# Splitting each 128x1024 weight tile with one ScalarE and one VectorE operation, two buffers each, in a two-layer hybrid model

## The chip, the core and the metric

The kernel runs on one core of one Trainium2 chip. The core has TensorE (PE, the matmuls; PEld is its loading of weights), VectorE (DVE), ScalarE (ACT), GpSimd (POOL) and SyncE (SP), whose queue issues the DMAs here. The engines run side by side, each through its own instructions in a fixed order, and wait for each other by semaphores. The metric is the device time of one execution in microseconds (us), as the median of several runs.

## What is computed

Two layers of a diffusion backbone on 256 context tokens and 256 latent tokens with 2048 channels. Cut to what matters (`ctx` and `x` are one array of 512 columns in the kernel):

```python
for l in range(2):
    u = rmsnorm(x, norm_w) * (1 + scale) + shift          # shift, scale, gate = silu(c) @ ada_w + ada_b
    lx, lg, q, k, v, ag, xbc, z, dt = split(u @ w_in)      # 2048 x 7184 weights
    lru = rglru(dwconv(lx)) * silu(lg)                     # two scans over the tokens
    att = window_attention(rope(rmsnorm(q)), rope(rmsnorm(k)), v) * silu(ag)
    ssd = rmsnorm(ssd_chunked(silu(dwconv(xbc)), dt) * silu(z))
    x = x + gate * (concat(lru, att, ssd) @ w_out)         # 3072 x 2048 weights
```

The second layer gives only the latent tokens. There the columns of `lg`, `q`, `ag`, `z`, `C` and the output projection are 256 wide; those of `B`, `x`, `lx`, `k`, `v`, and all of the first layer, are 512 wide.

## The kernel before

All weights are float32. To multiply them as float32r and keep their precision, each is split into two parts of 12 bits: `hi`, its value rounded by ScalarE into float32r, and `lo`, the rest, which VectorE subtracts. Each block of 128x128 weights then takes three matmuls in `mm3`: `hi` by `u_hi`, `hi` by `u_lo`, and `lo` by `u_hi`.

The weights lie in HBM as tiles of 128x1024 (512 KB), eight blocks each, in the order in which they are used: 112 tiles of `w_in` and 48 of `w_out` for each layer, 320 in all. The generator `blocks` streams them. For each tile it asks for a buffer `raw` (one of three), has SP load it (L232), and then for each of its two halves asks for a buffer `hi` and one `lo` (one of `HB` = 3 each, 128x512), gives ScalarE the rounding (L237) and VectorE the subtraction (L238), and yields the four blocks of the half. So 640 halves go through ACT and DVE. A buffer `hi` or `lo` comes free when TensorE is done with the half in it, a buffer `raw` when `lo` of its second half is computed. All matmuls go through L174; the three of a block are named `acc<-u,hi`, `acc<-u,hi` and `acc<-u,lo` (`mx` in place of `acc` for some column tiles).

`layer` runs, for each layer: the column tiles `B`, `C` and part of `x`, with the channel tiles outermost; the remaining `x`; eight pairs `lx`, `lg` (two tiles each), beside which the SSD's core runs; eight `z`; `k` and `v`; eight pairs `q`, `ag`; and the output projection in three thirds of 16 tiles each, one tile for one row block `m`, after which VectorE adds the gated result to `x` (L1073). The order of TensorE is that of the program: between two blocks `pump` puts in what the mixers need, when a clock of estimated matmul times says that it is due. The order on ACT, DVE, POOL and SP is set by a scheduler, which simulates the program when it is built; at run time each engine keeps to it. The mixers share those engines with the split: L380 (products for adaLN, on DVE, weights `araw` loaded by SP at L377), L1162 and L1166 (the SSD's weight matrices `ee`, `ww`), L730 to L735 (the LRU's scans), L650 and L654 (the gate of `z`), and loads and stores of `lru` and `att` through DRAM (L750, L900, L918, L1078).

Of the kernel before, what the change touches and what calls it, by code (L numbers as in the profile page):

```python
# [8 lines left out]
F32 = mybir.dt.float32  # L9
F32R = mybir.dt.float32r  # L10
AF = mybir.ActivationFunctionType
ALU = mybir.AluOpType
AX = mybir.AxisListType

P = 128
# [15 lines left out]
# The order in which the column tiles of w_in are multiplied: the first ones with the channel tiles outermost, those in  # L31
# FILL a few channel tiles at a time between them (in the first layer, whose adaLN weights take the DMAs' time).
HEAD = [[("B", 0), ("B", 1), ("C", 0), ("C", 1), ("x", 0), ("x", 1)]] * 2
FILL = [[("x", i) for i in range(2, 6)], []]
# [3 lines left out]
ROWS = (14, 11)  # the channel tiles multiplied one by one; the column tiles end one behind the other  # L38


def head_plan(l):
    """[(column tile, its channel tiles)] in order"""
# [21 lines left out]
def lead(at):  # L64
    """how many steps of the adaLN's rows go before the product of channel tile int(at)"""
    return int(np.interp(at, *LEAD)) // 2 * 2
# [26 lines left out]
OUT_PARTS = (0, 2, 1)  # lru, ssd, att: thirds of the rows of w_out  # L93
# [18 lines left out]
# Tiles of different phases that share their places.  # L112
SHARED = {}
for _tag, _bufs, _roles in [
        ("raw", 3, ("raw",)),
# [16 lines left out]
HB = 3  # L132
# [7 lines left out]
class Kernel:  # L140
# [52 lines left out]
    def wait(self, name):  # L193
        """how long, on TensorE's clock, to leave other engines for the step named"""
        return WAIT[name][self.l]
# [32 lines left out]
    def blocks(self, src, n_tiles):  # L228
        nc = self.nc
        for i in range(n_tiles):  # L230
            raw = self.t([P, 8, P], "raw")
            nc.sync.dma_start(out=raw, in_=src[i].rearrange("p (b c) -> p b c", b=8))  # L232
            for h in range(2):
                hi = self.t([P, 4, P], "hi", HB, F32R)
                lo = self.t([P, 4, P], "lo", HB, F32R)
                part = raw[:, 4 * h:4 * h + 4]
                nc.scalar.activation(out=hi, in_=part, func=AF.Copy)  # L237
                nc.vector.tensor_tensor(out=lo, in0=part, in1=hi.bitcast(F32), op=ALU.subtract)  # L238
                for b in range(4):
                    yield hi[:, b], lo[:, b]  # L240
# [8 lines left out]
    def setup(self):  # L249
# [25 lines left out]
        # 1/sqrt of the mean square of each token, on all partitions  # L275
# [1000 lines left out]
```

## Time and profile before

| | |
|---|---|
| median of 3 runs (lowest to highest) | 1871.07 us (1868.7 to 1872.88) |
| span of the profiled execution, the only time that its page gives | 1873.5 us |
| TensorE, matmuls | 1786.4 us busy, 95% |
| VectorE | 1474.5 us, 79% |
| ScalarE | 908.2 us, 48% |
| GpSimd | 438.0 us, 23% |
| mean granted TensorE clock | 0.981 of 2.4 GHz |

The busy share of TensorE is modelled from pipelined matmuls, so the idle time between them and the pace of a stream of blocks say more than the share. The stages differ in what is wide and what runs beside them, so the pace is read for each stage by itself.

### The profile page before, as it was taken

Reading aid. Unit: us, or ns where it says so; the run is one execution under the profiler, and the core shown is the slowest. Engines: PE = TensorE matmul, PEld = TensorE weight load, DVE = VectorE, ACT = ScalarE, POOL = GpSimd, SP = SyncE. Lnnn points to the kernel's source line nnn. Section 1 sums busy time; section 2 is a strip of 40 time slices with the busy share of each in tenths; the row PEclk is TensorE's granted clock in tenths of the full one; section 3 lists DMA queues with packets and bytes.
Section 4 is the critical chain, followed back from the end, with each engine's and each line's share of the span. In section 5 each row is a group of like instructions: output and inputs, shape, how many; then the busy total and the mean of one; then the engine's idle time right before and its main releaser. Section 6 shows DMA issues by size and latency. Waiting matters only on the chain.

```text
span 1873.5 us, 29483 instructions
## 1 busy us (share of the span) xinstructions
PE 1786.4 (95%) x10458; PEld 1493.3 (80%) x10458; DVE 1474.5 (79%) x3101; ACT 908.2 (48%) x1590; POOL 438.0 (23%) x467
## 2 busy tenths in 40 slices
PE   7999998887999999999999999999989899999999
PEld 4777876665767888887888887888767788999999
DVE  4447879899898888899999546877898895788765
ACT  4324565554633354546332234534656663677543
POOL 0000246665210022221100021011374430232000
PEclk9999999989999999999999998999999999999999
DMA  9982332333565655556766433354333555554666
GB/s 379 365 280 68 117 107 88 104 102 112 200 219 191 191 169 163 173 181 204 253 222 220 143 122 106 124 198 155 107 99 99 149 194 172 159 179 159 207 192 180
DMA packets 140259, 320.98 MB, mean 171 GB/s; under 512 B 14000, under 2 KB 41552, under 8 KB 139472
## 3 DMA queue, kind: packets, MB, share of 16 engines
q1 hardware_dynamic: 140112, 319.10, 52.0%
q8 instruction: 82, 1.34, 0.3%
q14 instruction: 65, 0.53, 0.1%
HBM read 308.41 MB, written 10.63 MB: 170 GB/s over the span
## 4 chain that ended last, share of the span: by engine, by line
PE 62%; DVE 10%; DMA 3%; issue 2%; ACT 2%; POOL 2%; SPq 0%; DVEq 0%; POOLq 0%; ACTq 0%
PE acc L174 52%; PE mx L174 8%; DVE lo L238 3%; DMA araw<-in_adaw_dram 1%; PE mx L170 1%; DVE ada L380 1%; DVE araw L380 1%; DVE ee L1162 1%; DVE ww L1166 1%; DMA raw<-in_w_in_dram 1%; POOL prob L864 0%; DMA bc<-acsD 0%; DVE xc L466 0%; ACT hi L237 0%; POOL ww L1164 0%
## 5 line engine op out<-in xcount | busy, mean ns | idle before, releaser
L174 PE MATMUL acc<-u,hi 128*128 128x512 f32 (+1 forms) x4800 | 1279.8, 355 | 8.6 <-ACT hi L237 4.2
L174 PEld LDWEIGHTS acc<-u,hi 128*128 128x128 f32 x4800 | 841.8, 191 | 135.0 <-issue 12.5
L174 PE MATMUL acc<-u,lo 128*128 128x512 f32 (+1 forms) x2400 | 847.6, 353 | 30.5 <-DVE lo L238 30.1
L237 ACT ACTIVATE hi<-raw 128x512 fp32r<-128x512 f32 x640 | 399.0, 628 | 607.6 <-PE acc L174 468.7
L238 DVE TENSOR_TENSOR lo<-raw,hi 128x512 fp32r<-128x512 f32 x640 | 471.9, 740 | 191.3 <-ACT hi L237 180.0
L174 PEld LDWEIGHTS acc<-u,lo 128*128 128x128 f32 x2400 | 457.3, 191 | 103.1 <-DVE lo L238 43.1
L380 DVE SCALAR_TENSOR_TENSOR araw<-araw,adac 128x512 f32<-128x512 f32 x256 | 187.0, 731 | 3.9 <-DMA araw<-in_adaw_dram 1.6
L380 DVE SCALAR_TENSOR_TENSOR ada<-araw,adac 128x512 f32<-128x512 f32 x192 | 146.4, 762 | 10.7 <-DMA araw<-in_adaw_dram 7.6
L427 POOL TENSOR_TENSOR ssq<-ssq,sq 128x512 f32<-128x512 f32 (+1 forms) x26 | 33.7, 1298 | 303.6 <-ACT sq L423 303.6
L864 POOL TENSOR_SCALAR prob<-prob,qrs 128x512 f32<-128x512 f32 (+1 forms) x48 | 60.8, 1279 | 187.4 <-ACT hi L237 142.6
L174 PE MATMUL mx<-u,hi 128*128 128x512 f32 (+1 forms) x320 | 99.7, 395 | 0.0
L1073 DVE SCALAR_TENSOR_TENSOR X<-acc,mod,X 128x256 f32<-128x256 f32 x144 | 65.2, 479 | 41.0 <-PE acc L174 40.7
L511 POOL TENSOR_SCALAR X<-xs,prm 128x512 f32<-128x512 f32 (+1 forms) x16 | 14.5, 908 | 323.3 <-DVE xs L489 323.3
L1174 POOL TENSOR_TENSOR bc<-bc,CT 128x512 f32<-128x512 f32 x40 | 59.3, 1483 | 37.4 <-ACT bc L1173 23.7
L174 PEld LDWEIGHTS mx<-u,hi 128*128 128x128 f32 x320 | 56.6, 191 | 14.1 <-issue 4.0
L1162 DVE SCALAR_TENSOR_TENSOR ee<-bc,nacs,ee 128x128 f32<-128x128 f32 x96 | 55.7, 624 | 14.8 <-DMA bc<-acsD 11.8
L767 POOL TENSOR_TENSOR qw<-qw,cst 128x256 f32<-128x256 f32 x20 | 22.4, 1118 | 191.3 <-DVE rt L766 122.1
L174 PE MATMUL mx<-u,lo 128*128 128x512 f32 (+1 forms) x160 | 61.0, 381 | 0.0
L1160 POOL TENSOR_SCALAR ee<-bc,nacs 128x128 f32<-128x128 f32 x96 | 50.0, 532 | 45.6 <-DMA bc<-acsD 31.6
L719 POOL TENSOR_TENSOR la<-lt 128x512 f32<-128x512 f32 x32 | 37.9, 1184 | 95.3 <-ACT lt L717 65.4
L727 POOL TENSOR_TENSOR lt<-lt,ltl 128x512 f32<-128x512 f32 x32 | 47.4, 1500 | 50.2 <-ACT ltl L724 36.3
L711 ACT ACTIVATE lt<-mx,gbh 128x512 f32<-128x512 f32 x64 | 43.0, 684 | 18.8 <-PE mx L174 18.1
(243 smaller groups left out, 2108.6 us busy)
## 6 DMA issues: line engine op xcount, KB each, us to landing
raw<-in_w_in_dram SPq DMA_DIRECT2D x224, 512.0 KB, 3.6
araw<-in_adaw_dram SPq DMA_DIRECT2D x256, 256.0 KB, 3.1
raw<-in_w_out_dram SPq DMA_DIRECT2D x96, 512.0 KB, 3.7
ar<-in_ada_dram SPq DMA_DIRECT2D x84, 256.0 KB, 5.9
bc<-acsD SPq DMA_DIRECT2D x48, 256.0 KB, 4.0
ar<-in_ada_dram SPq DMA_DIRECT2D x22, 512.0 KB, 7.3
adac<-condD SPq DMA_DIRECT2D x28, 256.0 KB, 4.8
X<-in_xT_dram SPq DMA_DIRECT2D x2, 2048.0 KB, 8.0
```

The source lines that it names most:

```text
L174: self.nc.tensor.matmul(out=out, lhsT=lhsT, rhs=rhs, start=start, stop=stop, **kw)
L237: nc.scalar.activation(out=hi, in_=part, func=AF.Copy)
L238: nc.vector.tensor_tensor(out=lo, in0=part, in1=hi.bitcast(F32), op=ALU.subtract)
L380: i = nc.vector.scalar_tensor_tensor(out=o, in0=raw, scalar=1.0, in1=row[c].rearrange("p t x -> p (t x)"), op0=ALU.mult, op1=ALU.mult, acc ...
L711: nc.scalar.activation(out=t, in_=pg, func=AF.Tanh, scale=0.5, bias=self.gb[:, 16 * g + 8 * d + m:16 * g + 8 * d + m + 1])
L719: nc.gpsimd.tensor_tensor(out=a2, in0=tr, in1=tr, op=ALU.mult)
L727: nc.gpsimd.tensor_tensor(out=ti, in0=ti, in1=tl[:, d], op=ALU.mult)
L864: nc.gpsimd.tensor_scalar(out=pr[j], in0=pr[j], scalar1=rs[:, j:j + 1], scalar2=1.0, op0=ALU.mult, op1=ALU.mult)
L1073: nc.vector.scalar_tensor_tensor(out=x[:, s], in0=acc[:, s.start - w0:s.stop - w0], scalar=mod[:, 2 * KT + m, c:c + 1], in1=x[:, s], op0=A ...
L1160: nc.gpsimd.tensor_scalar(out=e[:, j], in0=bcs[0][:, j], scalar1=1.0, scalar2=k.nacs[:, f:f + 1], op0=ALU.mult, op1=ALU.add)
L1162: nc.vector.scalar_tensor_tensor(out=e[:, j], in0=bcs[1][:, j], scalar=k.nacs[:, r:r + 1], in1=e[:, j], op0=ALU.add, op1=ALU.min)
L1174: nc.gpsimd.tensor_tensor(out=bc, in0=bc, in1=k.CT[:, g, None, tok].to_broadcast([P, 4, P]), op=ALU.mult)
```

## The change

The inner loop over halves goes. One operation of ScalarE rounds the whole 128x1024 tile, one of VectorE subtracts it, and the tile's eight blocks are yielded. The tiles `hi` and `lo` are twice as large and have two buffers (`HB` = 2) in place of three; `raw` has two in place of three. The space is the same: 3 x 4 KB + 2 x 3 x 2 KB = 24 KB a partition before, 2 x 4 KB + 2 x 2 x 4 KB = 24 KB after. The rest of the diff takes out comments and docstrings, which moves line numbers by up to two: L237, L238 of before are L235, L236 of after.

```diff
-        ("raw", 3, ("raw",)),
+        ("raw", 2, ("raw",)),
...
-HB = 3
+HB = 2
...
             nc.sync.dma_start(out=raw, in_=src[i].rearrange("p (b c) -> p b c", b=8))
-            for h in range(2):
-                hi = self.t([P, 4, P], "hi", HB, F32R)
-                lo = self.t([P, 4, P], "lo", HB, F32R)
-                part = raw[:, 4 * h:4 * h + 4]
-                nc.scalar.activation(out=hi, in_=part, func=AF.Copy)
-                nc.vector.tensor_tensor(out=lo, in0=part, in1=hi.bitcast(F32), op=ALU.subtract)
-                for b in range(4):
-                    yield hi[:, b], lo[:, b]
+            hi = self.t([P, 8, P], "hi", HB, F32R)
+            lo = self.t([P, 8, P], "lo", HB, F32R)
+            nc.scalar.activation(out=hi, in_=raw, func=AF.Copy)
+            nc.vector.tensor_tensor(out=lo, in0=raw, in1=hi.bitcast(F32), op=ALU.subtract)
+            for b in range(8):
+                yield hi[:, b], lo[:, b]
```

The matmuls and their order on TensorE stay. On the other engines the scheduler places things anew. On VectorE in the last third of the second layer's output projection there stood, for each tile `raw_N`, two halves and the gated addition of the tile before it (`acc`):

```order
L238 TENSOR_TENSOR lo_18508<-raw_18505,hi_18507 128x512
L238 TENSOR_TENSOR lo_18524<-raw_18505,hi_18523 128x512
L1073 SCALAR_TENSOR_TENSOR X_17111<-acc_18467,mod_33_146,X_17111 128x256
L238 TENSOR_TENSOR lo_18545<-raw_18542,hi_18544 128x512
L238 TENSOR_TENSOR lo_18561<-raw_18542,hi_18560 128x512
L1073 SCALAR_TENSOR_TENSOR X_17111<-acc_18504,mod_33_146,X_17111 128x256
```

Now there stands one subtraction for each addition:

```order
L236 TENSOR_TENSOR lo_17247<-raw_17244,hi_17246 128x1024
L1071 SCALAR_TENSOR_TENSOR X_16023<-acc_17210,mod_33_146,X_16023 128x256
L236 TENSOR_TENSOR lo_17280<-raw_17277,hi_17279 128x1024
L1071 SCALAR_TENSOR_TENSOR X_16023<-acc_17243,mod_33_146,X_16023 128x256
L236 TENSOR_TENSOR lo_17313<-raw_17310,hi_17312 128x1024
```

The addition for a tile keeps its place, ahead of the subtraction for the tile after the next.

On VectorE in the second layer's `z` tiles, where the LRU's last scans (`lh`), the gate of `z` (`cv`, then `X`) and the adaLN products (`araw`) share the engine, there stood before:

```order
L238 TENSOR_TENSOR lo_14614<-raw_14611,hi_14613 128x512
L650 SCALAR_TENSOR_TENSOR cv_14566<-cth_14565,acc_14496 128x256
L733 SCALAR_TENSOR_TENSOR lh_3050_14429<-lt_3045_14410,lt_3047_14416 128x256
L238 TENSOR_TENSOR lo_14630<-raw_14611,hi_14629 128x512
L654 SCALAR_TENSOR_TENSOR X_11270<-X_11270,cv_14566 128x256
L735 SCALAR_TENSOR_TENSOR lh_3050_14429<-lt_3045_14410,lh_3050_14429,lt_3047_14416 128x256
L238 TENSOR_TENSOR lo_14657<-raw_14654,hi_14656 128x512
L238 TENSOR_TENSOR lo_14673<-raw_14654,hi_14672 128x512
L380 SCALAR_TENSOR_TENSOR araw_14682,adas_11245<-araw_14682,adac_14026 128x512
L238 TENSOR_TENSOR lo_14694<-raw_14691,hi_14693 128x512
```

and for the same tiles now:

```order
L236 TENSOR_TENSOR lo_13714<-raw_13711,hi_13713 128x1024
L648 SCALAR_TENSOR_TENSOR cv_13670<-cth_13669,acc_13608 128x256
L731 SCALAR_TENSOR_TENSOR lh_2610_13549<-lt_2605_13530,lt_2607_13536 128x256
L652 SCALAR_TENSOR_TENSOR X_10594<-X_10594,cv_13670 128x256
L733 SCALAR_TENSOR_TENSOR lh_2610_13549<-lt_2605_13530,lh_2610_13549,lt_2607_13536 128x256
L236 TENSOR_TENSOR lo_13753<-raw_13750,hi_13752 128x1024
L378 SCALAR_TENSOR_TENSOR araw_13774,adas_10573<-araw_13774,adac_13174 128x512
L648 SCALAR_TENSOR_TENSOR cv_13742<-cth_13741,acc_13677 128x256
L652 SCALAR_TENSOR_TENSOR X_10594<-X_10594,cv_13742 128x256
L236 TENSOR_TENSOR lo_13786<-raw_13783,hi_13785 128x1024
```

What stood between two halves of a tile now stands between two whole tiles, four operations in a row.

On SP in the same place, with the loads of adaLN weights (`araw`) and of the stored `lru` (`ltl`, `stage`), there stood:

```order
L232 DMA raw_14654<-in_w_in_dram 128x1024
L377 DMA araw_14866<-in_adaw_dram 128x512
L232 DMA raw_14691<-in_w_in_dram 128x1024
L918 DMA ltl_16944<-lruD_11533 128x2x256
L918 DMA stage_16946<-lruD_11533 128x256
L232 DMA raw_14734<-in_w_in_dram 128x1024
L918 DMA stage_16948<-lruD_11533 128x256
```

and now, where `raw_13750` is the tile that was `raw_14654`, and `raw_13783` the one that was `raw_14691`:

```order
L232 DMA raw_13750<-in_w_in_dram 128x1024
L375 DMA araw_13942<-in_adaw_dram 128x512
L916 DMA ltl_15864<-lruD_10845 128x2x256
L916 DMA stage_15866<-lruD_10845 128x256
L232 DMA raw_13783<-in_w_in_dram 128x1024
L916 DMA stage_15868<-lruD_10845 128x256
```

The loads of weights slip back by about one tile among the other DMAs.

## Rows read from the trace of the kernel before

**Rows 1.** From the page: TensorE's busy line, and its granted clock in 40 slices.

```profile
PE 1786.4 (95%) x10458; PEld 1493.3 (80%) x10458; DVE 1474.5 (79%) x3101; ACT 908.2 (48%) x1590; POOL 438.0 (23%) x467
...
PEclk9999999989999999999999998999999999999999
```

**Rows 2.** Idle time by engine and releaser: us in total, times, longest us.

```profile
PE acc L174 <- DVE lo L238: 30.1, 27, 3.8
...
SPq L232 <- DVE lo L238: 745.7, 251, 12.3
```

**Rows 3.** Rounding (L237) by stretch: ACT busy (x operations), granted clock, DMA share, GB/s.

```profile
0.00:150.00 150.00, 20.07 (x32) 0.98 0.88 323
...
1498.00:1556.00 58.00, 20.68 (x34) 1.00 0.61 201
1603.00:1726.00 123.00, 40.02 (x64) 1.00 0.54 172
1750.00:1870.00 120.00, 50.98 (x81) 1.00 0.63 191
```

**Rows 4.** All engines by stretch: PE, PEld, DVE, ACT, POOL busy, clock, DMA share, GB/s.

```profile
260.00:600.00 340.00, 303.63 (x1453) 235.88 (x1451) 308.38 (x580) 163.02 (x252) 167.35 (x192) 0.95 0.45 146
...
1300.00:1498.00 198.00, 178.20 (x1024) 147.17 (x1023) 170.94 (x265) 123.86 (x193) 93.54 (x107) 0.96 0.36 115
1498.00:1556.00 58.00, 53.28 (x408) 50.53 (x408) 49.63 (x79) 38.09 (x65) 19.78 (x17) 1.00 0.61 201
```

**Rows 5.** Timeline, second layer's output projection: start us, us, engine, [idle before <-releaser].

```profile
1800.90 0.40 PE L174 MATMUL acc<-u,hi 128*128 128x256 f32 x2
...
1801.14 0.28 PE L174 MATMUL acc<-u,lo 128*128 128x256 f32 x1
...
1800.98 0.63 ACT L237 ACTIVATE hi<-raw 128x512 fp32r<-128x512 f32 x1 [0.81 <-PE acc L174]
1802.42 0.63 ACT L237 ACTIVATE hi<-raw 128x512 fp32r<-128x512 f32 x1 [0.81 <-PE acc L174]
...
1801.11 0.48 DVE L1073 SCALAR_TENSOR_TENSOR X<-acc,mod,X 128x256 f32<-128x256 f32 x1 [0.21 <-PE acc L174]
1801.65 0.69 DVE L238 TENSOR_TENSOR lo<-raw,hi 128x512 fp32r<-128x512 f32 x1
1803.09 0.69 DVE L238 TENSOR_TENSOR lo<-raw,hi 128x512 fp32r<-128x512 f32 x1 [0.75 <-ACT hi L237]
...
1795.17 29.13 SPq L232 DMA_DIRECT2D raw<-in_w_out_dram  x11
```

**Rows 6.** Groups by shape: busy us, mean ns; last row: 1498 to 1556 us.

```profile
L820 ACT ACTIVATE qh<-qw 128x512 fp32r<-128x512 f32 x8 | 5.0, 630 | 8.0 <-POOL qw L768 8.0
L820 ACT ACTIVATE qh<-qw 128x256 fp32r<-128x256 f32 x8 | 3.3, 416 | 5.8 <-POOL qw L768 5.8
...
L821 DVE TENSOR_TENSOR ql<-qw,qh 128x512 fp32r<-128x512 f32 x8 | 5.5, 683 | 0.0
L821 DVE TENSOR_TENSOR ql<-qw,qh 128x256 fp32r<-128x256 f32 x8 | 3.4, 424 | 2.2 <-ACT qh L820 2.2
...
L238 DVE TENSOR_TENSOR lo<-raw,hi 128x512 fp32r<-128x512 f32 x34 | 28.2, 843 | 7.8 <-ACT hi L237 7.8
```

**Rows 7.** DMA issues: KB each, median us to landing; page, then 1500 to 1556 us.

```profile
raw<-in_w_out_dram SPq DMA_DIRECT2D x96, 512.0 KB, 3.7
...
raw<-in_w_in_dram SPq DMA_DIRECT2D x17, 512.0 KB, 4.3
```

**Rows 8.** Timeline of ACT, first layer's output projection, 512 columns wide.

```profile
1071.12 0.63 ACT L237 ACTIVATE hi<-raw 128x512 fp32r<-128x512 f32 x1 [1.22 <-PE acc L174]
1073.83 0.63 ACT L237 ACTIVATE hi<-raw 128x512 fp32r<-128x512 f32 x1 [2.08 <-PE acc L174]
```

**Rows 9.** Timeline of DVE among the second layer's `z` tiles.

```profile
1530.24 2.30 DVE L730 TENSOR_TENSOR_SCAN lh<-lt,lt 128x512 f32<-128x512 f32 x1
1532.46 1.14 DVE L238 TENSOR_TENSOR lo<-raw,hi 128x512 fp32r<-128x512 f32 x1
...
1536.04 1.26 DVE L238 TENSOR_TENSOR lo<-raw,hi 128x512 fp32r<-128x512 f32 x2
```

## The prediction, made before the changed kernel was run

> **What bounds the kernel now.** I read the page's busy line first: TensorE is busy 95% of the span, and its granted clock stands at nine tenths or more in every slice [rows 1]. So the kernel is a stream of blocks through TensorE, and an edit to the splitting can only take away what TensorE waits for, or make it wait. The list of waits says how much there is to take: `acc` waits for `lo` 27 times, 30.1 us in all; the loads of `raw` wait on SP for `lo` 251 times, which is the queue waiting for a free buffer and costs nothing as long as the tile lands in time [rows 2]. The question is thus which of the rings of buffers is the next to be late, and that is read from one tile's timeline where nothing else runs.
>
> That place is the second layer's output projection [rows 5]. The roundings of two halves start 1.44 us apart, each released by TensorE, so a half takes 1.44 us and a tile of 256 columns 2.88; the eleven loads on SP stretch over 29.13 us, ten steps of 2.88 and one issue. A load goes out 0.03 us behind the subtraction of a second half (1803.09 + 0.69 = 1803.78, and 1795.17 + 3 x 2.88 = 1803.81). TensorE starts a half at 1800.90; the rounding into the buffer that this frees starts at 1800.98, and the subtraction follows 0.04 us behind it. With three halves, the subtraction ends at 1802.34 and the half is wanted two halves on, its first `lo` 0.24 us behind 1803.78: 1.68 us to spare. At 512 columns the roundings stand 2.72 us apart [rows 8], a tile takes 5.44 us.
>
> **The change part by part.**
>
> *The operations.* 640 roundings and 640 subtractions become 320 of each, twice as wide. From 256 to 512 columns a rounding goes from 416 to 630 ns and a subtraction from 424 to 683 [rows 6]; carried on by the same step for every 256 columns, 1024 take 630 + 2 x 214 = 1058 ns and 683 + 2 x 259 = 1201 ns, my estimates. VectorE saves 2 x 683 - 1201 = 165 ns a tile, 53 us in 320 tiles, at most; where two subtractions already run back to back they take 1.26 us together [rows 9], and the saving is 0.06 us, 19 us in all. It counts only where TensorE waits for VectorE. The stretches with such waits, 260 to 600 and 1300 to 1556 us, are 596 us of 1873 [rows 4], so it is worth between 0 and 53 x 596 / 1873 = 17 us. VectorE is busy 308 of 340 us there, that is, part of its time is waiting too; I take half of the lower price, 19 x 596 / 1873 / 2 = **3 us gained**.
>
> *Two buffers of whole tiles.* When TensorE starts a tile, the freed buffer now needs 1.06 + 0.04 + 1.20 = 2.30 us instead of 1.36 before its first `lo` can be used, and the time to spare in the place above falls from 1.68 to 1.68 - 0.94 = 0.74 us. At 512 columns 2.30 stands against 5.44 us, and an undisturbed stretch loses nothing. In return the second half of a tile can no longer be late by itself. Of the 27 waits for `lo` I put half, 15 us, to second halves: they go. The other 13 or 14 grow by up to 0.94 us: 12 us. As many places again, where there was less than 0.94 us to spare and no wait, come up with half of that each: 7 us. Sum of this part, in the stretches with the SSD's core, the LRU and the rest: **4 us lost**, between 15 gained (no growth) and 20 lost. The rows don't show how the waits divide, so both ends stay in the range. For the pairs `q`, `ag` (32 tiles in 123 us, 3.84 each [rows 3]) the same loss of margin at 256 columns, where VectorE has the queue of the attention, once in each of the eight pairs by 0.4 us: **3 us**, between 0 and 13 (once in each tile).
>
> *Two buffers for `raw`.* The wait on SP is now for the tile before the last, not the one before that. The ring of two: `lo` done, load issued 0.03 us later [rows 5], landed after 3.7 us [rows 7], rounding 1.06, 0.04, subtraction 1.20: 6.03 us for two tiles, 3.02 a tile. (The three-buffer ring of now, with halves, is some 5.8 us for three.) At 512 columns, 5.44 us, that is hidden; in the head, 32 halves in 150 us [rows 3], more so. At 256 columns it is longer than 2.88. In the output projection (81 halves in 120 us, with a few more ahead) the first six or so tiles live on the 0.74 us to spare, losing 0.27 for every two, and 35 more lose 0.14 each: **5 us lost**. If the loads landed in 3.4 us, it would be nothing (5.73 against 5.76); in the 4.3 us that they take among the `z` tiles [rows 7], 0.44 a tile, 17 us.
>
> In the `z` tiles (17 in 58 us, 3.41 each [rows 3]) the ring takes 0.03 + 4.3 + 1.06 + 0.04 + 1.48 = 6.91, where 1.48 is the subtraction at the 843 ns that a half takes there [rows 6], so 3.46 a tile: no slack at all. Everything that VectorE puts ahead of a subtraction there is added, and the order shows a scan, the gate and adaLN's product in front; the scan alone is 2.30 us [rows 9]. One operation of about 0.5 us in each ring of two gives 17 x (0.05 + 0.25) = 5; I take **4 us lost**, between 0 and 12 (two or three operations). Behind SP's longer waits stand the loads of `araw`, `ltl` and `stage`; their users on VectorE and ScalarE then hold up the next subtraction, which is part of the same bound.
>
> A rule weighed: here the two-deep ring of loads is 3.02 us against a tile of 2.88. The Trainium skill, in "Trainium Kernel Development and Optimization", section "Best Practices", advises to double-buffer for performance, so that DMA overlaps with compute; by it two buffers would be enough, and the two terms for `raw`, 5 and 4 us, would be nothing.
>
> *Sum.* 5 + 4 + 3 + 4 - 3 = 13 us. The page gives no time around the span of 1873.5; the runs' median lies 2.4 us below it, and I take the change onto the median: 1871.1 + 13 = **1884 us**. TensorE's clock is granted at 0.95 in 260 to 600 us and 0.96 in 1300 to 1498 [rows 4], in the stretches where it waits, and other waits will move that by a few us either way.
>
> **The rivals.**
>
> *Both rings are covered, 1871 us.* Loads land in 3.4 us, for there are fewer at a time, and the vanished waits of second halves pay for the rest. For it: 0.74 us are left, and 3.7 is a median, with shorter ones among it. Against it: SP's loads stand exactly 2.88 us apart, so few overlap now, and 3.7 is nearly the time of a lone one.
>
> *VectorE's saving wins, 1857 us.* The 15 us of second-half waits go, first halves don't grow because VectorE, with 320 instructions less, is earlier by the 0.06 to 0.165 us a tile (6 us where it counts); against it only the two rings of `raw`, 5 and 2 us: 1871 + 7 - 21 = 1857. It decides if VectorE is what TensorE waits for in 260 to 600 and 1300 to 1556 us. For it: VectorE busy 308 of 340 us there, PE 304 [rows 4]. Against it: VectorE is idle for 32 us of that stretch itself, so it is the order of its work, not its rate, that is late. The Trainium skill has this as a rule, in "VectorE: DVE Perf Modes", section on the TRN2 errata: operations from SBUF pay a fixed latency for each instruction, which one large tile pays once. The trace agrees with a fixed part of 165 ns or less in each subtraction.
>
> *The ring of `raw` binds wherever 256 columns are, 1906 us.* With loads at 4.3 us throughout: 17 in the output projection, 12 in `z`, 6 in `q`, `ag`: 35 us. For it: SP keeps one order, and a load behind a late `araw` is later still. Against it: in 1750 to 1870 us SP carries little but weights.
>
> That the change doesn't do what it says is none: the order has 320 operations of 128x1024 on each engine.
>
> **How the numbers follow.** The forecast, 1875 to 1900 us, has 0.52; covered 0.15; VectorE's saving 0.17; the ring everywhere 0.16. Faster or slower is meant by over 0.2%, 3.7 us, about what a measurement of this kernel can tell from no change: faster 0.17, same 0.15, slower 0.68. The range of 8 in 10 reaches from 1860, into the third case, to 1906, the middle of the fourth.
>
> **What would show it.** In the output projection of the second layer the loads on SP should start about 3.0 us apart instead of 2.88, TensorE should wait for `lo` or ScalarE for the landing of `raw` a little in each tile, and the stretch that took 120 us should take 125. Rounding and subtraction should take 1.06 and 1.20 us. In the `z` tiles the ring should be seen at 3.5 us a tile or more. At 512 columns (1060 to 1150 us) nothing should move. The number of waits for `lo` should fall and their mean grow. It is wrong if the loads land faster with two buffers, if the waits for `lo` in the SSD's stretches shrink by more than 10 us, or if the schedule of those stretches changes TensorE's idle time by more than the terms here.

## The result, and the profile after

| | before | after |
|---|---|---|
| median (lowest to highest) | 1870.56 us (1868.7 to 1872.88) | 1901.7 us (1896.64 to 1905.72) |
| span of the profiled execution | 1873.5 us | 1894.9 us |
| ratio of after to before | | 1.0162, 95% interval 1.0141 to 1.0184 |

The change makes the kernel 31 us slower; forecast were 13. The direction and the main place were right, the size was not. The profiled execution of after is the lowest of its four runs (1896.64 us), and that of before has a span (1873.5 us) longer than each of before's four times; so the two traces show 21 of the 31 us.

The page of after, its first lines (engine, busy us, share, instructions), the shares of the chain of work that ended last, and the two groups that the change made (count, busy us, mean ns):

```profile
PE 1792.7 (95%) x10458; PEld 1493.1 (79%) x10458; DVE 1441.2 (76%) x2781; ACT 855.1 (45%) x1270; POOL 450.8 (24%) x467
...
PE 58%; DVE 18%; DMA 9%; ACT 6%; issue 4%; POOL 4%; SPq 0%; ACTq 0%; POOLq 0%; DVEq 0%
...
L235 ACT ACTIVATE hi<-raw 128x1024 fp32r<-128x1024 f32 x320 | 338.5, 1058 | 594.2 <-PE acc L174 334.2
...
L236 DVE TENSOR_TENSOR lo<-raw,hi 128x1024 fp32r<-128x1024 f32 x320 | 409.8, 1281 | 167.0 <-ACT hi L235 165.9
```

VectorE is 33 us less busy (1474.5 before), ScalarE 53 (908.2), and neither helps: TensorE's share is the same 95% of a longer span [rows 1]. DMA and DVE have grown in the chain (3% and 10% before). Who waits is in the list of waits of after (who waited for whom: us in total, times, longest us), to be read against [rows 2]:

```profile
ACT hi L235 <- DMA raw<-in_w_out_dram: 78.9, 35, 6.2
PEld acc L174 <- DVE lo L236: 61.7, 59, 4.0
...
PE acc L174 <- DVE lo L236: 43.4, 40, 3.6
...
ACT hi L235 <- DMA raw<-in_w_in_dram: 25.3, 15, 4.3
```

TensorE's 27 waits of 30.1 us for `lo` have become 40 of 43.4. The first line has no counterpart of that size before: ScalarE now waits 35 times for weights of the output projections to land.

By stage, from the first weight load of a stage's first tile on TensorE to that of the next stage (of the last one to the end of the span), read from the two traces (us):

| | before | after | difference | forecast |
|---|---|---|---|---|
| layer 1, all | 1126.1 | 1118.8 | -7.3 | part of +4 and -3 |
| layer 2: first column tiles | 66.8 | 67.0 | +0.2 | 0 |
| layer 2: remaining `x` | 69.8 | 75.1 | +5.3 | part of +4 and -3 |
| layer 2: `lx`, `lg` | 210.7 | 209.4 | -1.3 | part of +4 and -3 |
| layer 2: `z` | 56.3 | 60.8 | +4.5 | +4 |
| layer 2: `k`, `v` | 48.9 | 48.9 | 0 | 0 |
| layer 2: `q`, `ag` | 123.0 | 127.9 | +4.9 | +3 |
| layer 2: output projection | 146.7 | 162.2 | +15.5 | +5 |

So the error of the forecast sits first of all in the last line. In that stretch ScalarE and VectorE of after look like this (timelines: start us, us, instruction, in brackets the idle time before it and what ended it), where [rows 5] showed roundings released by TensorE:

```profile
1804.47 1.06 ACT L235 ACTIVATE hi<-raw 128x1024 fp32r<-128x1024 f32 x1 [3.71 <-DMA raw<-in_w_out_dram]
1806.12 1.06 ACT L235 ACTIVATE hi<-raw 128x1024 fp32r<-128x1024 f32 x1 [0.59 <-DMA raw<-in_w_out_dram]
1810.47 1.06 ACT L235 ACTIVATE hi<-raw 128x1024 fp32r<-128x1024 f32 x1 [3.30 <-DMA raw<-in_w_out_dram]
```

```profile
1800.79 1.23 DVE L236 TENSOR_TENSOR lo<-raw,hi 128x1024 fp32r<-128x1024 f32 x1 [0.83 <-ACT hi L235]
...
1805.56 1.23 DVE L236 TENSOR_TENSOR lo<-raw,hi 128x1024 fp32r<-128x1024 f32 x1 [2.52 <-ACT hi L235]
1806.70 0.48 DVE L1071 SCALAR_TENSOR_TENSOR X<-acc,mod,X 128x256 f32<-128x256 f32 x1
1807.21 1.23 DVE L236 TENSOR_TENSOR lo<-raw,hi 128x1024 fp32r<-128x1024 f32 x1
...
1811.56 1.23 DVE L236 TENSOR_TENSOR lo<-raw,hi 128x1024 fp32r<-128x1024 f32 x1 [1.31 <-ACT hi L235]
```

One turn of the ring can be read off. The subtraction that starts at 1800.79 ends at 1802.02, and SP issues the next load then; the tile has landed for the rounding at 1806.12 (the buffer of the tile rounded at 1804.47 is the other one), and its subtraction ends at 1807.21 + 1.23 = 1808.44: 6.42 us for two tiles. The other buffer's turn goes from 1806.79 to 1812.79, 6.00 us. Two tiles of TensorE's work are 5.76 us. TensorE shows the gap on the tile that comes late (its timeline):

```profile
1805.58 0.50 PE L174 MATMUL acc<-u,hi 128*128 128x256 f32 x2 [0.19 <-ACT hi L235]
1806.84 0.39 PE L174 MATMUL acc<-u,lo 128*128 128x256 f32 x1 [0.76 <-DVE lo L236]
```

### The profile page after: what moved, and what is told of

It reads as the page before. It is cut to its first block, busy times and chain, and to the rows that moved or that the text cites. A ratio compares the mean times of both kernels' runs of the same rounds, so it can differ in the third digit from the quotient of the medians.

```text
span 1894.9 us, 28229 instructions
## 1 busy us (share of the span) xinstructions
PE 1792.7 (95%) x10458; PEld 1493.1 (79%) x10458; DVE 1441.2 (76%) x2781; ACT 855.1 (45%) x1270; POOL 450.8 (24%) x467
## 4 chain that ended last, share of the span: by engine, by line
PE 58%; DVE 18%; DMA 9%; ACT 6%; issue 4%; POOL 4%; SPq 0%; ACTq 0%; POOLq 0%; DVEq 0%
PE acc L174 43%; PE mx L174 12%; DVE lo L236 5%; DMA raw<-in_w_out_dram 4%; PE ada L174 2%; ACT hi L235 2%; DVE ee L1160 2%; DMA araw<-in_adaw_dram 1%; DVE ww L1164 1%; DVE araw L378 1%; DMA raw<-in_w_in_dram 1%; PE mx L170 1%; DMA bc<-acsD 1%; DVE ada L378 1%; POOL prob L862 1%
## 5 line engine op out<-in xcount | busy, mean ns | idle before, releaser
L174 PE MATMUL acc<-u,lo 128*128 128x512 f32 (+1 forms) x2400 | 852.1, 355 | 44.5 <-DVE lo L236 43.4
L235 ACT ACTIVATE hi<-raw 128x1024 fp32r<-128x1024 f32 x320 | 338.5, 1058 | 594.2 <-PE acc L174 334.2
L236 DVE TENSOR_TENSOR lo<-raw,hi 128x1024 fp32r<-128x1024 f32 x320 | 409.8, 1281 | 167.0 <-ACT hi L235 165.9
L378 DVE SCALAR_TENSOR_TENSOR ada<-araw,adac 128x512 f32<-128x512 f32 x192 | 142.1, 740 | 10.4 <-DMA araw<-in_adaw_dram 6.3
L425 POOL TENSOR_TENSOR ssq<-ssq,sq 128x512 f32<-128x512 f32 (+1 forms) x26 | 41.3, 1590 | 299.1 <-ACT sq L421 298.1
L1158 POOL TENSOR_SCALAR ee<-bc,nacs 128x128 f32<-128x128 f32 x96 | 58.1, 619 | 42.6 <-DMA bc<-acsD 34.7
```

Of the source, the lines that this page charges most:

```text
L174: self.nc.tensor.matmul(out=out, lhsT=lhsT, rhs=rhs, start=start, stop=stop, **kw)
L235: nc.scalar.activation(out=hi, in_=raw, func=AF.Copy)
L236: nc.vector.tensor_tensor(out=lo, in0=raw, in1=hi.bitcast(F32), op=ALU.subtract)
L378: i = nc.vector.scalar_tensor_tensor(out=o, in0=raw, scalar=1.0, in1=row[c].rearrange("p t x -> p (t x)"), op0=ALU.mult, op1=ALU.mult, acc ...
L425: nc.gpsimd.tensor_tensor(out=self.ssq[0], in0=self.ssq[0], in1=sq, op=ALU.add)
L1158: nc.gpsimd.tensor_scalar(out=e[:, j], in0=bcs[0][:, j], scalar1=1.0, scalar2=k.nacs[:, f:f + 1], op0=ALU.mult, op1=ALU.add)
```

## The experiments

Each kernel was timed beside the kernel before on the same chip; its medians there were 1874.1 to 1874.6 us (1870.6 beside the change itself). The ratios:

| kernel | raw | hi, lo | operations | ratio to before (95% interval) |
|---|---|---|---|---|
| before | 3 tiles | 3 halves | 128x512 | 1 |
| raw 2 | 2 tiles | 3 halves | 128x512 | 1.0128 (1.0111 to 1.0145) |
| raw 2, four halves | 2 tiles | 4 halves | 128x512 | 1.0079 (1.0053 to 1.0104) |
| changed, halved operations | 2 tiles | 2 tiles | 128x512 | 1.0082 (1.0066 to 1.0099) |
| the change | 2 tiles | 2 tiles | 128x1024 | 1.0162 (1.0141 to 1.0184) |
| changed, third raw tile in the last third | 2, then 3 tiles | 2 tiles | 128x1024 | 1.0156 (1.0135 to 1.0177) |
| changed, no loads in layer 2 | 2 tiles | 2 tiles | 128x1024 | 1.0148 (1.0134 to 1.0162) |
| before, no loads in layer 2 | 3 tiles | 3 halves | 128x512 | 1.0093 (1.0079 to 1.0107) |
| halves throughout, six and three | 6 halves | 3 halves | 128x512 | 1.0004 (0.9995 to 1.0014) |
| halves throughout, four each | 4 halves | 4 halves | 128x512 | 0.9961 (0.9949 to 0.9974) |
| mixed: layer 1 changed, layer 2 before | | | | 1.0014 (0.9999 to 1.0028) |
| mixed: layer 1 raw 2 and four halves, layer 2 before | | | | 1.0098 (1.0084 to 1.0111) |

And the stages that differ (us, as in the table above):

| kernel | layer 1 | `x` | `lx`, `lg` | `z` | `q`, `ag` | output projection | its last third |
|---|---|---|---|---|---|---|---|
| before | 1126.1 | 69.8 | 210.7 | 56.3 | 123.0 | 146.7 | 49.7 |
| the change | 1118.8 | 75.1 | 209.4 | 60.8 | 127.9 | 162.2 | 55.1 |
| raw 2 | 1127.5 | 70.0 | 213.0 | 60.6 | 127.8 | 157.4 | 52.9 |
| raw 2, four halves | 1122.0 | 69.5 | 209.8 | 60.4 | 123.6 | 158.6 | 54.4 |
| halved operations | 1122.8 | 74.5 | 209.2 | 60.5 | 126.8 | 151.1 | 51.6 |
| third raw tile at the end | 1123.2 | 77.1 | 213.3 | 61.3 | 128.1 | 159.6 | 49.7 |
| changed, no loads | 1124.3 | 75.3 | 228.1 | 59.0 | 127.9 | 146.5 | 49.5 |
| before, no loads | 1125.6 | 69.6 | 227.0 | 57.6 | 123.0 | 146.6 | 49.5 |
| halves, six and three | 1121.5 | 70.4 | 212.9 | 55.3 | 123.0 | 147.1 | 49.9 |
| halves, four each | 1121.4 | 70.3 | 206.8 | 53.0 | 123.6 | 147.0 | 49.7 |
| mixed, changed first | 1128.2 | 71.0 | 211.7 | 56.3 | 123.0 | 147.6 | 49.7 |
| mixed, four halves first | 1134.7 | 73.8 | 210.7 | 56.3 | 123.0 | 148.0 | 49.7 |

The columns `z`, `q`, `ag` and output projection are steady: kernels that share a scheme there agree within some 1.3 us, apart from the first two thirds of the output projection with a ring that is too long. Layer 1, `x` and `lx`, `lg` move by several us from kernel to kernel, and not only because the scheduler's order is new: the change and the kernel with a third raw tile have the same order on ScalarE, VectorE and GpSimd up to the output projection of layer 2, and their traces differ by 4.4, 2.0 and 3.9 us in these three columns. There is one trace for each kernel, so differences of that size in these columns show no cause.

**1. Two raw buffers alone.** The kernel before, with one number changed:

```diff
-        ("raw", 3, ("raw",)),
+        ("raw", 2, ("raw",)),
```

> The kernel before with two buffers for the raw tiles in place of three; halves, three buffers hi and lo, all else as before. Theory 1 (the ring of two raw tiles with its load costs the second layer's 256-column stages): the ring is 0.03 + 3.9 (mean landing) + 0.10 + 0.63 + 0.04 + 0.68 + 0.68 = 6.06 us for two tiles, 3.03 a tile against 2.88, so the output projection of layer 2 takes 7 us more (146.8 to 154), z and q, ag some 2 us each: about 1882 us. Theory 2 (the coarser grain of hi and lo, whole tiles with 2.3 us from TensorE's release to lo, is the cause): within 3 us of before, about 1871 us, the output projection still 2.88 us a tile. Theory 3 (the scheduler's new order is the cause): no stage moves by its ring, a few us either way anywhere.

Measured: 1896.4 us. The output projection takes 157.4 us (+10.7; theory 1 had +7), `z` +4.3 and `q`, `ag` +4.8. Theory 2 is refuted as the whole cause: without any merging, 24 us are lost (by the ratio; the medians differ by 22). The loads on SP in the output projection, in before, after and this kernel (a tile's view over that stretch: instruction, count, duration in ns, first and last start; then the landing):

```profile
L232 SPq DMA_DIRECT2D raw<-in_w_out_dram x44: 327/328/333, 1732.0 to 1858.5; - x44
DMA to landing us min/median/max: 3.2/3.7/6.7
```

```profile
L232 SPq DMA_DIRECT2D raw<-in_w_out_dram x45: 327/328/333, 1736.6 to 1882.3; - x45
DMA to landing us min/median/max: 3.2/3.7/6.6
```

```profile
L232 SPq DMA_DIRECT2D raw<-in_w_out_dram x45: 327/328/333, 1745.5 to 1885.7; - x45
DMA to landing us min/median/max: 3.5/3.8/7.4
```

First to last, the loads stand 126.5 / 43 = 2.94 us apart before, 145.7 / 44 = 3.31 after, and 140.2 / 44 = 3.19 with two raw tiles and halves. The landing itself is nearly the same in all three: what differs is whether it is hidden.

**2. Two raw buffers and four halves**, the memory of the changed kernel without the merging:

```diff
-        ("raw", 3, ("raw",)),
+        ("raw", 2, ("raw",)),
...
-HB = 3
+HB = 4
```

> The kernel before with two raw buffers and four buffers each of hi and lo halves: the same 24 KB as the changed kernel, and the same memory held, only in halves. What is between it and the changed kernel is the merging of the operations alone. Theory 1: the ring of raw is as in the kernel with raw 2, 6.06 us for two tiles: output projection of layer 2 about 154 us, 1882 us in all; the changed kernel's 6.36 us ring is 0.15 us a tile dearer, because a whole tile must be rounded before anything of it is subtracted. Theory 2: halves, so no loss, 1871 us or, with one more buffer, 2 to 5 us less.

Measured: 1886.6 us, between the two. The output projection is no better for the fourth half (158.6 us), since the ring of raw does not pass through it; `q`, `ag` come back to 123.6; layer 1 is 4 us faster, which is no more than one trace can differ from another there. So a fourth half hides late loads in `q`, `ag`, where there is slack, and none where the ring itself is too long.

**3. A third raw tile, late.** The changed kernel, with a buffer that the attention has left, for every third raw tile in the last 16 tiles:

```diff
-            raw = self.t([P, 8, P], "raw")
+            raw = self.t([P, 8, P], "raw3" if third and i >= third and i % 3 == 2 else "raw")
...
-        ("t4", 3, ("BT", "CT", "Btok", "vh", "vl", "ptlh", "ar0")),
+        ("t4", 3, ("BT", "CT", "Btok", "vh", "vl", "ptlh", "ar0", "raw3")),
...
-        wo = self.blocks(self.a["w_out"][l], 48)
+        wo = self.blocks(self.a["w_out"][l], 48, 32 * l)
```

> The changed kernel with every third raw tile of the last third of layer 2's output projection in a buffer that the attention has left: there the ring is of three raw tiles, hi and lo stay two whole tiles. Theory 1: three tiles for 6.36 us, 2.12 a tile, so TensorE's 2.88 sets the pace again: the last third goes from 55.1 us to about 50, the kernel from 1901.7 to 1896.5 us. Theory 2 (the ring of hi and lo sets the pace): the last third stays at 55 us, the kernel at 1901.7.

Measured: the last third goes from 55.1 to 49.7 us, exactly that of before. ScalarE's timeline in the second third (two raw tiles) and in the last (three):

```profile
1837.08 1.06 ACT L235 ACTIVATE hi<-raw 128x1024 fp32r<-128x1024 f32 x1 [2.52 <-DMA raw<-in_w_out_dram]
1839.66 1.06 ACT L235 ACTIVATE hi<-raw 128x1024 fp32r<-128x1024 f32 x1 [1.53 <-DMA raw<-in_w_out_dram]
```

```profile
1865.89 1.06 ACT L235 ACTIVATE hi<-raw 128x1024 fp32r<-128x1024 f32 x1 [1.82 <-PE acc L174]
1868.77 1.06 ACT L235 ACTIVATE hi<-raw 128x1024 fp32r<-128x1024 f32 x1 [1.82 <-PE acc L174]
```

The same operations and the same two whole tiles of `hi` and `lo` now stand 2.88 us apart and are released by TensorE. The landings in the last third were no shorter (median 4.4 us). So with three raw tiles the wide operations and the whole tiles of `hi` and `lo` cost nothing here; what binds with two is the ring of raw as a whole, its operations included (experiment 5). The whole kernel did not gain the 5 us (1902.3 us, ratio 1.0156 against 1.0162): `x`, `lx`, `lg` and the first two thirds of the output projection of its profiled execution were 9 us longer, so this verdict rests on the stage alone.

**4. No loads of weights in layer 2**, in the changed kernel and, as a control, in the one before:

```diff
+            if self.l and i >= n_raw:
+                raw = raws[i % n_raw]
+            else:
...
+                raws.append(raw)
```

> The changed kernel without the loads of weights in the second layer: all but the first two tiles of each of its two streams are left out, and the raw tiles loaded first are split again and again (so layer 2 computes with wrong weights). The rounding, the subtraction and the two buffers of hi and lo stay. Theory 1 (the loss is the landing inside the ring of two raw tiles): the output projection of layer 2 goes from 162.2 us back to about 147, q, ag from 127.9 to 123, z from 60.8 to 57, the x tiles keep their 5 us: about 1876 us. Theory 2 (whole tiles in hi and lo, 2.3 us from TensorE's release to lo, are late by themselves): the output projection stays above 152, and the kernel above 1885 us.

> The control to the one above: the kernel before without the loads of weights in the second layer, all but the first three tiles of each stream (layer 2 computes with wrong weights). Both theories: the ring of three raw halves' tiles was hidden, so no stage of layer 2 gains more than 1 us and the kernel stays at 1868 to 1874 us. If it gains more, loads of before were late in places that the waits put down to another engine.

Measured: 1902.2 us, and 1891.9 in the control. The output projection is at 146.5 us without the loads (146.6 in the control). With two whole tiles of `hi` and `lo` and operations of 1024 columns, TensorE runs at its own pace there. So all 15.5 us need the loads in the ring: without them the wide operations cost nothing there. `q`, `ag` stay at 127.9, the same as with the loads, and `x` at 75.3: that part is no matter of loads, and theory 1 was wrong on `q`, `ag`. `z` gives back 1.8 of 4.5 us.

Both kernels missed their expected totals for another reason: `lx`, `lg` of layer 2 took 16 us more in the control and 19 more in the changed kernel. In the control's list of waits from 1288 to 1396 us:

```profile
PEld mx L174 <- ACT bdh L699: 14.3, 2, 9.3
...
ACT bdh L699 <- DMA gw<-in_gates_dram: 11.5, 2, 8.3
```

TensorE waits for the LRU's gate weights, whose load (`gw`) landed late twice; in before, no such wait is in the list of that stretch. A kernel with other loads gets another order from the scheduler. That the place of `gw` in SP's order made them late was not tried.

**5. The operations alone.** The changed kernel with its buffers, but two operations for each tile on each engine:

```diff
-            nc.scalar.activation(out=hi, in_=raw, func=AF.Copy)
-            nc.vector.tensor_tensor(out=lo, in0=raw, in1=hi.bitcast(F32), op=ALU.subtract)
-            for b in range(8):
-                yield hi[:, b], lo[:, b]
+            for h in range(2):
+                p = slice(4 * h, 4 * h + 4)
+                nc.scalar.activation(out=hi[:, p], in_=raw[:, p], func=AF.Copy)
+                nc.vector.tensor_tensor(out=lo[:, p], in0=raw[:, p], in1=hi[:, p].bitcast(F32), op=ALU.subtract)
+                for b in range(4 * h, 4 * h + 4):
+                    yield hi[:, b], lo[:, b]
```

> The changed kernel with its buffers (two whole tiles each of raw, hi and lo), but with two roundings and two subtractions of 512 columns a tile in place of one of 1024. Without the loads of layer 2 the changed kernel's output projection came back to 146.5 us and z to 59.0, but its x tiles (75.3) and its q, ag (127.9) stayed as slow as with them. Theory 2a (what stays is the operations of 1024 columns: mixers' work behind them in VectorE's order is late): x goes back to 70 and q, ag to 123 to 124; the ring of raw is 0.03 + 3.96 + 0.10 + 0.63 + 0.04 + 0.68 + 0.68 = 6.12 us for two tiles, 3.06 a tile, so the output projection takes 155 instead of 162: in all about 1884 us. Theory 2b (it is the release of whole tiles): x 75 and q, ag 128 us as in the changed kernel, about 1895.

Measured: 1888.3 us, ratio 1.0082, between the two theories. With these buffers the merging thus costs (1.0162 - 1.0082) x 1874 = 15 us; the two traces show 9 of them, and 11.1 in the output projection (162.2 against 151.1), where halving the operations shortens the ring: the subtraction of the first half runs beside the rounding of the second. `x` (74.5) and `q`, `ag` (126.8) stay, as theory 2b had it. VectorE's timeline shows the ring's tail here, and beside it the one of the kernel with raw 2 and four halves:

```profile
1804.60 1.29 DVE L238 TENSOR_TENSOR lo<-raw,hi 128x512 fp32r<-128x512 f32 x2 [1.20 <-ACT hi L237]
1805.82 0.48 DVE L1073 SCALAR_TENSOR_TENSOR X<-acc,mod,X 128x256 f32<-128x256 f32 x1
```

```profile
1804.49 0.69 DVE L238 TENSOR_TENSOR lo<-raw,hi 128x512 fp32r<-128x512 f32 x1 [1.80 <-ACT hi L237]
1805.10 0.48 DVE L1073 SCALAR_TENSOR_TENSOR X<-acc,mod,X 128x256 f32<-128x256 f32 x1
1805.49 0.68 DVE L238 TENSOR_TENSOR lo<-raw,hi 128x512 fp32r<-128x512 f32 x1
```

In the second the scheduler put the gated addition between the two subtractions: 0.4 us in each turn of the ring (6.48 against 6.09 us in the mean of tiles 276 to 317, landings 3.99 and 3.96), which accounts for its output projection of 158.6 in place of 151.1 us. So what the merging costs here hangs on that order: with the addition in between, halves have no shorter ring than whole tiles. In the second and last thirds that kernel is as slow as the change (105.8 against 106.0 us), and its 3.6 us less are nearly all in the first.

**6. Halves throughout.** Loads of 256 KB, a buffer of raw for each half; four buffers each (24 KB), and as a control six of raw and three each of `hi` and `lo` (24 KB as well):

```diff
-            raw = self.t([P, 8, P], "raw")
-            nc.sync.dma_start(out=raw, in_=src[i].rearrange("p (b c) -> p b c", b=8))
             for h in range(2):
...
-                part = raw[:, 4 * h:4 * h + 4]
+                part = self.t([P, 4, P], "raw")
+                nc.sync.dma_start(out=part, in_=src[i].rearrange("p (b c) -> p b c", b=8)[:, 4 * h:4 * h + 4])
```

> Halves throughout, the raw weights too: loads of 128x512 (256 KB), four buffers each of raw, hi and lo halves, 24 KB as in both kernels. Theory 1: the ring is 0.03 + 3.4 (the 256 KB loads of adaLN weights land in 3.3) + 0.10 + 0.63 + 0.04 + 0.68 = 4.88 us for four halves, 1.22 a half against TensorE's 1.44, so the second layer is as before (output projection 147 us), though raw has 8 KB as in the changed kernel; the first layer keeps the 4 us of the kernel with four halves: about 1867 to 1870 us. Rival (the bytes in the ring count, not the steps: 8 KB of raw are too few): output projection 154 us or more, 1885 us.

> Halves throughout with loads of 256 KB, but six buffers of raw halves and three each of hi and lo, which is the memory of the kernel before (12 + 12 KB). The kernel with four of each ran 8 us faster than before. If the fourth half of hi and lo gives that (theory 2: VectorE's margin in the first layer's z and the second's lx, lg and z): no gain here, 1872 to 1876 beside before at 1874. If the finer loads give it (a half can be rounded as soon as its own 256 KB have landed): about 1867 us here too.

Measured: 1866.5 us with four each, the fastest kernel of the study (ratio 0.9961, 0.9949 to 0.9974); 1875.6 with six and three, the same as before. With the 8 KB of raw that the change has, the output projection is at 147.0 us: 8 KB of raw are enough when they are cut into four steps. The landing in that stretch, ScalarE's timeline there, and TensorE's waits for `lo` in the whole kernel:

```profile
DMA to landing us min/median/max: 2.5/3.0/6.0
```

```profile
1790.67 0.63 ACT L236 ACTIVATE hi<-raw 128x512 fp32r<-128x512 f32 x1 [0.81 <-PE acc L174]
1792.11 0.63 ACT L236 ACTIVATE hi<-raw 128x512 fp32r<-128x512 f32 x1 [0.81 <-PE acc L174]
```

```profile
PEld acc L174 <- DVE lo L237: 15.4, 20, 2.0
PE acc L174 <- DVE lo L237: 9.2, 11, 1.8
```

Roundings 1.44 us apart, released by TensorE, and 11 waits for `lo` of 9.2 us in place of 27 of 30.1 [rows 2]. The control, with 25 such waits of 31.2 us, shows that the fourth half gives this, not the finer loads; the finer loads make room for it. By stage the gain over before is in the second layer's `lx`, `lg` (-3.9) and `z` (-3.3) and in layer 1 (-4.7); but the control has the -4.6 of layer 1 too without being faster as a whole, so that part is not the fourth half's.

**7. Two mixed kernels**, in which the same six buffers of 4 KB are cut one way in layer 1 and another in layer 2:

```diff
+            if self.l == MERGED:
+                a, b = ("wa", "wb") if i % 2 == 0 else ("wb", "wa")
+                raw = self.t([P, 8, P], a, 3)
...
+                hi = self.t([P, 8, P], a, 3, F32R)
+                lo = self.t([P, 8, P], b, 3, F32R)
...
+            raw = self.t([P, 8, P], "wa", 3)
...
+                both = self.t([P, 2, 4, P], "wb", 3, F32R)
+                hi, lo = both[:, 0], both[:, 1]
```

> The changed scheme (whole tiles, two buffers each) in the first layer, the one of before (three raw, three halves) in the second, in the same 24 KB. By stage the changed kernel gained 8 us in layer 1 and lost 29 in layer 2. Theory 1 (the loss belongs to 256 columns): the second layer is back to the times of before, the first keeps the gain: 1871 - 8 = 1863 us. Theory 3 (both are accidents of the scheduler's order): layer 1 does not keep the 8 us, 1867 to 1875 us.

> Two raw tiles and four halves in the first layer, three raw tiles and three halves in the second, in the same 24 KB. In the kernel with raw 2 and four halves layer 1 was 4 us faster than before, by -6.5 in the later lx, lg, -1.6 in z, +3.0 in k, v. Theory 1 (a fourth half is worth that where VectorE is late): 1874 - 4 = 1870 us beside before at 1874. Theory 3 (order by chance, as the 7 us that the first tiles lost in the mixed kernel): 1872 to 1880 us, with other stages moving.

Measured: 1874.9 us, the same as before, and 1891.8 us. Theory 1 holds for layer 2, whose `z`, `q`, `ag` are at 56.3 and 123.0 in both. The gain of layer 1 did not come along: 1128.2 and 1134.7 us instead of 1118.8 and 1122.0. Theory 3 was right in that the gain did not last; the second kernel's 1891.8 us lie above what either theory gave it (1870, and 1872 to 1880). In the first, 7 us are lost in the first 20 weight tiles (169.7 us, before 162.7); what in the order of the shared buffers did that was not found.

## Why the prediction was right in direction and wrong in size

**The output projection, the step that failed.** The mechanism, the place and the sign were right: the ring of two raw tiles binds there. The term was +5 and measured +15.5. The sum 0.03 + 3.7 + 1.06 + 0.04 + 1.20 = 6.03 us was too small in its landing, which was a median, and had no hand-over from the landing to the rounding; and one price was taken for all tiles. In the trace of after the loss falls into two parts (tiles counted from 0 over both layers; the projection begins with tile 272).

The first 4.6 us are lost on tiles 272 to 277. Two loads of weights, issued at 1741.03 and 1742.80 us, landed after 6.6 and 6.4 us; SP had issued a load of 1 MB of `X` just before them. ScalarE waits, and TensorE waits 3.5 us for what comes of these two tiles and the next:

```profile
1739.93 0.43 SPq L1053 DMA_DIRECT2D X<-xD  x1
1741.03 0.33 SPq L232 DMA_DIRECT2D raw<-in_w_out_dram  x1
...
1747.69 1.06 ACT L235 ACTIVATE hi<-raw 128x1024 fp32r<-128x1024 f32 x1 [6.17 <-DMA raw<-in_w_out_dram]
...
1748.80 0.50 PE L174 MATMUL acc<-u,hi 128*128 128x256 f32 x2 [1.97 <-ACT hi L235]
```

Before has two such loads (6.7 and 6.4 us) behind the same load of `X`, and with its third buffer TensorE keeps to 2.88 us on their tiles. That the load of `X` makes them late was not tried. No term of the prediction has them. From tile 278 to 286 nothing is lost.

The other 10.4 us are the term itself. From the times of each load, rounding and subtraction over tiles 287 to 318 of after: issue 0.03 us behind the subtraction, landing 3.91, from the landing to the rounding 0.14, from there to the end of the subtraction 2.34: 6.42 us for two tiles. The excess over 5.76 is 0.66 and not 0.27, and 32 tiles x 0.33 = 10.6 us. Of the 0.39 that the sum missed, 0.21 are the landing, 0.14 the hand-over and 0.04 the operations; the count of tiles (35) was about right. The median landing, 3.7, is still that of after over the whole stretch, but the mean counts where no load that is late can be won back. In before's own trace the mean could have been read: its loads in that stretch went from 3.2 to 6.7 us, with a mean of 3.9. With it alone the same working gives 6.23 us and some 8 us lost.

The whole is 18 us above the forecast by the medians. The traces show about half of that: the projection is 10.5 us above its term, `q`, `ag` 1.9 and `z` 0.5, and layer 1, `x` and `lx`, `lg` together are 3.3 us faster where +1 was forecast. The other 10 of the 31 us are in no stage of the two traces, and where they arise is open.

**`z`: +4 forecast, +4.5 measured.** Two raw tiles alone give +4.3. Without loads the changed kernel is still 2.7 us above before, but the control 1.3 as well; so some 1.4 us, a third of it, may be VectorE's work in front of the subtraction, and that is no more than such stages differ from kernel to kernel. The ring of raw, which the step named, is shown; its part for VectorE's queue is not.

**`q`, `ag`: +3 forecast, +4.9 measured, and not by the loads.** The step said loss of margin in VectorE's queue, because the wider operations take 2.30 in place of 1.36 us. That it is not the loads holds: 127.9 us with and without them. That it is the wider operations is not shown: with halved operations in the same buffers the stage is still at 126.8. And part of what is late is not `lo`. In after's `q`, `ag`, from 1621 to 1749 us:

```profile
PEld mx L174 <- DVE ql L819: 3.1, 6, 1.1
...
PEld acc L174 <- DVE lo L236: 2.1, 3, 0.9
```

In before there were 2 such waits for `ql`, 0.7 us. With four halves of `hi` and `lo` in place of two whole tiles the stage is at 123.6. The same 4.8 us in the kernel with raw 2 and three halves have another cause, the loads: there ScalarE waits ten times, 12.0 us, for `raw`.

**Waits for `lo` elsewhere: +4 forecast.** The mean grew, as forecast (1.1 to 1.2 us), but the number did not fall: outside the output projection 27 waits became 31, and 30.1 us became 37.9. Half of the waits were put to second halves that would go; the count shows no such gain. The clearest new ones are in the `x` tiles of layer 2, +5.3 us, which no step had by itself. There the SSD's core starts, and its work stands ahead of the split on VectorE (after):

```profile
1253.29 2.36 DVE L1160 SCALAR_TENSOR_TENSOR ee<-bc,nacs,ee 128x128 f32<-128x128 f32 x4 [2.44 <-DMA bc<-acsD]
1255.57 1.52 DVE L464 SCALAR_TENSOR_TENSOR cv<-acc,scwh,cv 128x510 f32<-128x510 f32 x2
1257.01 2.28 DVE L236 TENSOR_TENSOR lo<-raw,hi 128x1024 fp32r<-128x1024 f32 x1
```

TensorE waits for this `lo` and then 2.5 us for `xs`, which stands behind it. Two kernels that differ in the buffers' grain (whole tiles against four halves, both with operations of 512 columns) have `x` at 74.5 and 69.5 us. But a mixed kernel with before's halves and buffers in layer 2 has it at 73.8, so a like rise comes without that grain. Whether the grain itself or the order that the scheduler builds from it does this was not separated.

**VectorE's saving: -3 forecast, none seen.** The durations were right: 1.058 and 1.281 us in the mean (1.226 undisturbed) for 1.06 and 1.20, and VectorE is 33 us less busy. But the kernel with halved operations and the same buffers is 15 us faster. In layer 1, where the ring is hidden, it is 3.3 us faster than before, and the three kernels with merged operations and these buffers 7.3, 2.9 and 1.8, though these three have the same order there almost to the layer's end: a gain of a few us is possible, its size is not to be told from such traces. The rival built on it (1857) falls: TensorE's waits for `lo` did not shrink, though VectorE was less busy.

**At 512 columns with nothing beside them** nothing moved, as forecast: the output projection of layer 1 and `k`, `v` of layer 2 differ by less than 1 us.

**The rivals.** "Both rings are covered" (1871) falls with experiment 1. The Trainium skill, in "Trainium Kernel Development and Optimization", section "Best Practices", advises to double-buffer so that DMA overlaps with compute. For these loads two buffers were not enough: with the third one taken away, and nothing else changed, the kernel lost 24 us. "The ring binds wherever 256 columns are" (1906) has the nearest number; of its 17 us in the output projection 15.5 came, of its 12 in `z` 4.5.

**A reading that was wrong.** The prediction took TensorE's granted clock to be at nine tenths or more in every slice. In [rows 1] two of the 40 slices show 8, that is between 80% and 90%; nothing in its sum hangs on it.

**The sum.** Step by step in ratios: raw from three to two +24 us, the fourth half -9, whole tiles in place of four halves about +1, merged operations +15; in all 1.0162 x 1874 - 1874 = 30 us. The steps are differences between kernels whose orders differ too, as the gated addition in experiment 5 shows. The range (1860 to 1906) held the 1901.7, by a rival's price and not by the forecast's working.

## What to carry to other kernels

Before taking a buffer from a ring of loads, add up one turn of it (issue, landing, hand-over, every operation until the buffer is free) with the mean landing and not the median, and set it against as many tiles of the bounding engine as there are buffers; where the turn is longer, every late load is lost for good. Look also for the places where other large loads go out beside the ring: two late loads made 4.6 of the 15.5 us here. A merged operation can lengthen each ring it stands in by the part that two halves would have overlapped, as long as nothing is put between the halves. Smaller pieces in more buffers, in the same bytes, were the faster direction here.

## What the runs showed of the hardware that was not expected

Loads of 256 KB land only a little sooner than loads of 512 KB: minimum and median 2.5 and 3.0 us against 3.2 and 3.7, on the same queue and in the same stretch. So most of the landing did not go with the size here, and four small buffers hid more of it than two large ones (output projection 147.0 against 158.6 us, both with four halves of `hi` and `lo`). The Trainium skill, in "DMA: Bandwidth & Descriptors", section "Anatomy of one DMA — SWDGE (gpsimd) path", fits 2.0 us and 436e3 bytes for each us more: that would be 2.6 and 3.2 us. These runs, on SP's queue, agree with it for the fastest loads, and their means are 0.7 us longer (3.26 and 3.96 over the 96 and 48 loads of the stretch).

The subtraction that took 2.28 us above, against 1.23 elsewhere, ran while GpSimd multiplied `bc` by `CT` (1256.92 to 1260.42 us in its timeline). The Trainium skill, in the specifications table of "GPSIMD Engine Reference", says that GpSimd shares its SBUF interfaces with VectorE and contends with instructions of two SBUF inputs; the trace agrees, with a factor of 1.9 here. Of the 320 subtractions of after, the 228 with no GpSimd operation beside them took 1.16 to 1.23 us, the other 92 up to 2.31 us. This one comes at the place where `lo` was already late.

Taking loads away made a stage slower by 16 us (experiment 4). With an order that is fixed when the program is built, less work is another order, and a control that leaves work out has to be read by stage.
